# Input projections and GLA of a hybrid diffusion step: from the scheduler's order to an order by program

## The chip, the cores and the metric

The kernel runs on one core of a Trainium2 chip. The metric is device time in microseconds (us) of one execution. Before the change, three runs took 972.02, 972.9 and 973.95 us; the median is 972.9. The engines of a core work side by side, each through its own queue in order: TensorE (PE in the profile, PEld for its weight loads), VectorE (DVE), ScalarE (ACT), GpSimd (POOL), and SyncE (SP), which issues the DMA transfers.

## The reference

One trunk layer for 256 prompt tokens and 1024 latent tokens, width 1024. Each token is RMS-normalised, shifted and scaled by a conditioning vector, and multiplied by one input matrix of 3616 columns. Two head groups read the result.

```python
p = einsum('bld,dp->blp', h, w_in)           # GLA q, k, v, low-rank decays; diff q, k, v; gates
# GLA, forward and backward, chunks of 64 tokens
b = cumsum(g); o = (q * exp(b)) @ S + att @ v            # att: decayed q k^T inside the chunk
S = exp(b_last) * S + (k * exp(b_last - b)).T @ v
# differential attention: two softmax maps per head, keys: cache of 512 + latent (rotary), or prompt
a = softmax(q1 k1) - lam * softmax(q2 k2); o = a @ v
y = x + gate * (concat(rmsnorm(o_gla), rmsnorm(o_diff)) * silu(g)) @ w_out      # then a final rmsnorm
```

Outputs: both token groups, the prompt's diff keys and values, and its two GLA states.

## The kernel before

All float32 products are made from two rounded parts: a tile is split into `hi` (rounded to fp32r) and `lo` (the remainder, rounded), and three matmuls are summed: hi*hi, hi*lo, lo*hi. A weight "unit" is 128 x 1024 values: 128 output features by 1024 inputs, or half of a 256-feature block by tokens.

The program has four stages. The start (`START`, an order written by hand) makes the modulation vectors and the normalised, transposed, split tokens `hhi`, `hlo`, and projects three units. Then come the projections and GLA, which the change rewrites. Attention follows with 16 blocks, again in a hand-written order (`ORDER`), and then the output projection.

The middle part is written as Python generators that `mix` (L102) interleaves by a string: "m" takes one step of the main generator (the projections), "a", "b" and "c" one step of the others. There are three strings, `MIX[0]` to `MIX[2]`. Without `manual_schedule`, this order is only a priority: the framework's scheduler orders each engine's instructions by its own estimate of when they can run. In `START` and `ORDER`, inside `manual_schedule`, TensorE, VectorE, ScalarE and GpSimd execute in the order in which the program issues; SyncE's queue stays with the scheduler in all stages.

- Main steps. `feat_unit` (L462) loads and splits one weight unit and multiplies it with three token blocks of 256, 512 and 512 columns (`feat_block`, L445); it yields after every second of the eight inner tiles for 512 columns, after every fourth for 256. `tok_block` (L518) loads two units and goes over ten tiles of 128 tokens with 256 columns each, in two steps per tile; the first step uses the first unit, the second step the second. Each block ends with a consumer that evicts the accumulator (three buffers, `psA`): `use_kq`, `use_gv`, `use_dv`, `use_dqk` (rotary) and `use_gate` (silu by Abs, Exp, Ln, min and subtract, Exp, multiply).
- `load_unit` (L249) issues the load of a weight unit and its split at the place of use. `WENG` says by which engines: "G" GpSimd alone, "V" GpSimd rounds and VectorE subtracts, "A" ScalarE and GpSimd, "B" ScalarE and VectorE.
- `MIX[0]`, the decay stage: GLA queries and values; beside them `decays` (L982), `modgate` (L695, gate row of the modulation, on VectorE) and `wo_parts` (L681, splitting the output weights in 16 parts and storing them in device memory).
- `MIX[1]`, the gate stage: gates 0 to 3; beside them `pass_a` (L730, forward GLA states, chunk by chunk: multiply on GpSimd, transposes, ScalarE copy, state matmuls) and `cached` (L667, splitting cached keys and values).
- `MIX[2]`: diff values, keys and queries and the gates 4 to 7; beside them the backward GLA pass `pass_b` (L951), the prompt's heads (`prompt`, L992), the loads of the first attention block, and its scores (`first_block`, L1280) through one PSUM buffer.

In `pass_b` a pair of chunks takes eight steps. Step s does `product(s)` on TensorE (`lv`, two double PSUM banks), `grow` (VectorE multiplies, one ScalarE copy) and `select` (VectorE copies where a mask holds). Beside step s, stage s of the pair before is finished: `turn`, `states`, `output`, then `square` and `norm` for each chunk, which read the output `op` from its PSUM bank.

Of the kernel before, what the change touches and what calls it, by code (L numbers as in the profile page):

```python
# [19 lines left out]
P = 128  # L20
D = 1024
# [80 lines left out]
def mix(pattern, main, *others):  # L102
# [4 lines left out]
    for g in gens.values():  # L107
# [14 lines left out]
    ('mmmmabmmmmammammbmammmmamcmmmacbmbbcmmmmcmambcambmcmmmacmmmbcmmmbcmmbmcamamcammbcmmbbcmmabcmmamcammm'  # L122
     'cmmbmm'),
    ('mmamamaaammaaabmmmmaaammaaambmmaammabmabaammaambamammbmmabammmmabammmamamaaaammabaabmaamma'),
    ('ammmmmmammammamaamammammmmaammammmammmamammammmmmammmmaammmmmmammmmammmamamamammmaammammmammmmmmamam'
     'aammmmmamammmammmammammmmmammmmaammmamammmaamammammmmmammammammmmaamammmmaaammmaaaammaaammmmamaamaaa'
     'mmamaaamaammaaamaaammamamamaaamaaamammmaaaamaamaaaaaamaammmmaaamammaammmamm'),
# [51 lines left out]
def body(tc, nc, I, O, ctx):  # L179
# [57 lines left out]
    with psum:  # L237
# [9 lines left out]
        nload = [0]  # L247

        def load_unit(u):  # L249

            raw = wp.tile([P, D], F32, name="w_raw", tag="wr", bufs=2)
            S.dma_start(raw, I["w_u"][u])
            hi = wp.tile([P, D], F32R, name="w_hi", tag="wh")
            lo = wp.tile([P, D], F32R, name="w_lo", tag="wl")
            how = WENG[nload[0]]
            nload[0] += 1
            if how in "AB":
                A.activation(hi, raw, AF.Copy)
            else:
                G.tensor_scalar(out=hi, in0=raw, scalar1=1.0, scalar2=0.0, op0=ALU.mult, op1=ALU.add)  # L260
            (V if how in "BV" else G).tensor_tensor(out=lo, in0=raw, in1=hi.bitcast(F32), op=ALU.subtract)  # L261
            return hi, lo
# [33 lines left out]
        class Start:  # L296
# [146 lines left out]
        sp = proj.enter_context(tc.tile_pool(name="sp", bufs=2, side="right"))  # L443

        def feat_block(w, bi, consumer, s0=0, n=0):  # L445
# [39 lines left out]
        U_LR, U_K, U_Q, U_G, U_DK, U_DQ, U_GV, U_DV = 0, 1, 3, 5, 13, 17, 21, 25  # L485
# [32 lines left out]
        def tok_block(u, consumer, tiles=range(NCH)):  # L518
            w2 = [load_unit(u), load_unit(u + 1)]
            for t in tiles:  # L520
# [3 lines left out]
                for kt in range(KT):  # L524
# [8 lines left out]
                    if kt == 3:  # L533
                        yield
# [4 lines left out]
        def decay(bi, c0, n):  # L539

            nch, ch0 = n // P, c0 // P
            for dr in range(2):
                for pr in range(2):
# [10 lines left out]
                    G.tensor_tensor(out=mn, in0=mn, in1=la, op=ALU.subtract)  # L554

# [55 lines left out]
        def use_dqk(isk, pair, v):  # L611
# [6 lines left out]
            def f(bi, c0, n, ps):  # L618
# [23 lines left out]
                split_store(ua, dst(0), col, n, scale, engine(e + 4))  # L642
# [3 lines left out]
                split_store(ub, dst(1), col, n, scale, engine(e + 4))  # L646
            return f

        def use_gate(m):
            gn = vecs[:, V_GG:V_GG + 1] if m < 4 else vecs[:, V_DG:V_DG + 1]  # L650

            def f(bi, c0, n, ps):
# [6 lines left out]
                A.activation(ls, ls, AF.Exp)  # L659
                gt = sp.tile([P, 512], F32, name="gt", tag="s3")[:, :n]  # L660
                V.scalar_tensor_tensor(out=gt, in0=ps, scalar=gn, in1=ls, op0=ALU.mult, op1=ALU.mult)
                S.dma_start(gt_d[m, :, c0:c0 + n], gt)
                if bi == 0:
                    gated.add(m)
            return f

        def cached():  # L667
            for pair in range(2):
                for v in range(2):
                    r = sp.tile([P, 512], F32, name="kqst", tag="s1")  # L670
                    S.dma_start(r, I["ck"][pair, v])
                    split_store(r, [ks_d[pair][0, v], ks_d[pair][1, v]], 0, PAST, 1.0, G)
                    yield
            for t in range(4):
                r = sp.tile([P, 512], F32, name="kqst", tag="s1")
                S.dma_start(r, I["cv"][t * P:(t + 1) * P])
                rows = vs_d[:, t * P:(t + 1) * P]
                split_store(r, [rows[0], rows[1]], 0, 512, 1.0, G)
                yield

        def wo_parts():  # L681

            for i in range(16):
                m, cs, odd = i // 2, slice(i % 2 * 512, i % 2 * 512 + 512), i % 2
                r = gp.tile([P, 512], F32, name="wor", tag="kk", bufs=2)
                S.dma_start(r, I["w_out"][SLOT[m] * P:(SLOT[m] + 1) * P, cs])
# [6 lines left out]
                yield  # L693

        def modgate():  # L695
# [3 lines left out]
            for kt in range(KT):  # L699
                wg = gp.tile([P, 2, 512], F32, name="wg", tag="att", bufs=2)  # L700
                for hf in range(2):
                    S.dma_start(wg[:, hf], I["w_mod"][kt * P:(kt + 1) * P, 2 * D + hf * 512:2 * D + (hf + 1) * 512])
                for j in range(2):
                    for hf in range(2):
# [8 lines left out]
            for j in range(2):  # L713
                for hf in range(2):
                    cs = slice(hf * 512, (hf + 1) * 512)
                    ps = psL.tile([P, 2, 512], F32, name="gs", tag="lv")[0:1, 0]
                    T.matmul(ps, one, acc[j][hf], start=True, stop=True)
                    row = sp.tile([1, 512], F32, name="grow", tag="s2")
                    S.dma_start(row, I["bgate"][:, cs])
                    V.tensor_tensor(out=row, in0=ps, in1=row, op=ALU.add)  # L720
                    S.dma_start(ga_d[j:j + 1, cs], row)
                    yield
# [7 lines left out]
        def pass_a():  # L730

            cur = None
            for c in range(NCH - 1):
                x = gp.tile([P, 6, 256], F32, name="fa", tag="W", bufs=2)
                k, to, ks, v, kt_ = x[:, 0], x[:, 1], x[:, 2], x[:, 3:5].rearrange("p a b -> p (a b)"), x[:, 5]
                S.dma_start(x[:, 0:1].rearrange("p a (b t) -> p (a b) t", t=P), kq_d[c, :, 0:2])
                S.dma_start(x[:, 1:2].rearrange("p a (b t) -> p (a b) t", t=P), e_d[c, :, 4:6])
                S.dma_start(v, gv_d[c * P:(c + 1) * P])
# [29 lines left out]
        class Pair:  # L768
# [151 lines left out]

            def square(self, i):
                op = self.op[:, :, i * 256:(i + 1) * 256]
                self.sq = gp.tile([P, 512], F32, name="sq")
                A.activation(self.sq.rearrange("p (a b) -> p a b", a=2), op, AF.Square)
                self.sqh = gp.tile([P, 512], F32R, name="sqh", tag="hi")
                G.tensor_scalar(out=self.sqh, in0=self.sq, scalar1=1.0, scalar2=0.0, op0=ALU.mult, op1=ALU.add)
                self.sql = gp.tile([P, 512], F32R, name="sql", tag="lo")
                G.tensor_tensor(out=self.sql, in0=self.sq, in1=self.sqh.bitcast(F32), op=ALU.subtract)

            def norm(self, i):  # L930

                c, rs = 2 * self.p + i, self.sq
                ms = psX.tile([P, 512], F32, name="ms", tag="aux")
                T.matmul(ms, onesr, self.sqh, start=True, stop=False)
# [617 lines left out]
```

## Time and profile before

| | before |
|---|---|
| median of three runs | 972.9 us |
| the profiled execution | 980.17 us, span 978.4 us |
| busy PE / DVE / ACT / POOL | 908.9 / 609.0 / 467.1 / 424.5 us |
| mean granted clock of TensorE | 0.983 |
| DMA | 174.71 MB, mean 179 GB/s |

The span runs from the first to the last instruction. Busy times are shares of that span; idle time of an engine that does not set the pace costs nothing. A matmul's end is modelled, so consecutive matmuls overlap in the record, and the start-to-start distance is the better measure of their pace. The clock is the TensorE clock that was granted: 1.00 is 2.4 GHz and 0.50 is 1.2 GHz.

### The profile page before, as it was taken

To read this page: it belongs to the slowest core of one execution; us is meant where nothing else is said; L and a number is where in the kernel's file an instruction comes from. 1 tells how busy PE (TensorE), PEld (TensorE's weight loads), DVE (VectorE), ACT (ScalarE), POOL (GpSimd) and SP (SyncE) were. 2 spreads that over 40 slices of the span, in tenths; PEclk is the share of its full clock that TensorE was granted. 3 is DMA by queue.
4 is the path that set the end of the run, shared out by engine and by line. 5 is a ranking of instruction groups with operands and counts; after the bars stand their busy time and mean duration, and the time that the engine had idled before them with its cause. 6 is when DMAs were issued, how large, how long until landed. Compare 5 with 4: busy or idle time off the path is not lost. (4 is left out here: it accounts for less than half of the span.)

```text
span 978.4 us, 16000 instructions
## 1 busy us (share of the span) xinstructions
PE 908.9 (93%) x5894; PEld 768.7 (79%) x5894; DVE 609.0 (62%) x837; ACT 467.1 (48%) x893; POOL 424.5 (43%) x349
## 2 busy tenths in 40 slices
PE   6889989899898999889899999899999999999997
PEld 1379878687688988677777888778888888887886
DVE  3688874224337664678766653789999999522223
ACT  2455445525452232324233475678888888521212
POOL 0253544532520312342314300079999999942221
PEclk9889999999999999999999999999999999999999
DMA  7851878788873635255437437397533426037941
GB/s 273 310 173 40 262 230 272 241 270 264 276 244 100 194 120 178 73 168 175 134 120 232 151 121 245 121 312 236 151 99 126 120 71 204 23 108 226 285 130 65
DMA packets 155535, 174.71 MB, mean 179 GB/s; under 512 B 11192, under 2 KB 116792, under 8 KB 155456
## 3 DMA queue, kind: packets, MB, share of 16 engines
q1 hardware_dynamic: 155456, 173.69, 56.1%
q8 instruction: 46, 0.75, 0.4%
q14 instruction: 33, 0.27, 0.1%
HBM read 112.69 MB, written 60.96 MB: 177 GB/s over the span
## 5 line engine op out<-in xcount | busy, mean ns | idle before, releaser
L454 PE MATMUL acc<-hhi,w_hi 128*128 128x512 f32 (+1 forms) x440 | 157.8, 359 | 0.0
L455 PE MATMUL acc<-hlo,w_hi 128*128 128x512 f32 (+1 forms) x440 | 155.6, 354 | 0.0
L456 PE MATMUL acc<-hhi,w_lo 128*128 128x512 f32 (+1 forms) x440 | 155.3, 353 | 0.0
L1153 DVE TENSOR_REDUCE sm<-sc 128x1 f32<-128x1536 f32 x60 | 104.8, 1749 | 9.3 <-PE sc L1146 9.3
L1197 POOL TENSOR_TENSOR aTl<-aT,aTh 128x512 fp32r<-128x512 f32 x80 | 107.7, 1354 | 6.4 <-ACT aTh L1192 1.0
L1146 PE MATMUL sc<-ks,q 128*128 128x512 f32 x360 | 99.4, 412 | 2.7 <-ACT p L1158 2.7
L1158 ACT ACTIVATE p<-sc,sm 128x1536 f32<-128x1536 f32 x60 | 92.6, 1544 | 16.0 <-DVE sm L1153 14.7
L530 PE MATMUL acc<-w_hi,hhi 128*128 128x256 f32 x320 | 94.6, 296 | 6.1 <-ACT kqst L479 4.1
L531 PE MATMUL acc<-w_lo,hhi 128*128 128x256 f32 x320 | 92.7, 290 | 0.9 <-DVE w_lo L261 0.9
L454 PEld LDWEIGHTS acc<-hhi,w_hi 128*128 128x128 f32 x440 | 83.2, 189 | 12.8 <-issue 1.8
L532 PE MATMUL acc<-w_hi,hlo 128*128 128x256 f32 x320 | 92.5, 289 | 0.0
L456 PEld LDWEIGHTS acc<-hhi,w_lo 128*128 128x128 f32 x440 | 83.1, 189 | 11.6 <-issue 0.2
L455 PEld LDWEIGHTS acc<-hlo,w_hi 128*128 128x128 f32 x440 | 83.4, 189 | 10.6 <-issue 0.3
L1194 POOL TENSOR_SCALAR aTh<-aT 128x512 fp32r<-128x512 f32 x64 | 62.4, 975 | 36.1 <-ACT aT L1183 30.3
L1146 PEld LDWEIGHTS sc<-ks,q 128*128 128x128 f32 x360 | 64.0, 191 | 15.1 <-ACT p L1158 3.0
L530 PEld LDWEIGHTS acc<-w_hi,hhi 128*128 128x128 f32 x320 | 63.2, 197 | 12.4 <-ACT kqst L479 4.3
L1168 DVE SCALAR_TENSOR_TENSOR p<-p,sm,p 128x1536 f32<-128x1536 f32 x30 | 70.1, 2338 | 1.1
L1363 PE MATMUL sc<-woh,oh 128*128 128x512 f32 (+1 forms) x168 | 65.0, 387 | 0.9 <-DVE y__9404 L1368 0.9
L1364 PE MATMUL sc<-wol,oh 128*128 128x512 f32 (+1 forms) x168 | 64.5, 384 | 0.0
L1365 PE MATMUL sc<-woh,oh 128*128 128x512 f32 (+1 forms) x168 | 64.5, 384 | 0.0
L531 PEld LDWEIGHTS acc<-w_lo,hhi 128*128 128x128 f32 x320 | 63.2, 198 | 1.6 <-DVE w_lo L261 1.1
L1177 PE MATMUL tp<-ident,p 128*128 128x128 f32 x360 | 58.3, 278 | 6.4 <-DVE p L1168 3.5
(308 smaller groups left out, 2110.3 us busy)
## 6 DMA issues: line engine op xcount, KB each, us to landing
w_raw<-w_u SPq DMA_DIRECT2D x29, 512.0 KB, 5.2
oh<-oh_d SPq DMA_DIRECT2D x20, 512.0 KB, 6.4
wm<-w_mod SPq DMA_DIRECT2D x16, 512.0 KB, 6.4
q<-qs_d SPq DMA_DIRECT2D x64, 128.0 KB, 2.8
ks<-ks_d SPq DMA_DIRECT2D x4, 1536.0 KB, 7.6
vs<-vs_d SPq DMA_DIRECT2D x8, 768.0 KB, 7.5
xt<-x_all SPq DMA_DIRECT2D x10, 512.0 KB, 10.2
x<-x_all SPq DMA_DIRECT2D x10, 512.0 KB, 4.6
```

The lines of the kernel that those rows point to most:

```text
L454: T.matmul(ps, w_h, hhi[bi][:, kt, ts], start=kt == 0, stop=False)
L455: T.matmul(ps, w_h, hlo[bi][:, kt, ts], start=False, stop=False)
L456: T.matmul(ps, w_l, hhi[bi][:, kt, ts], start=False, stop=kt == KT - 1)
L530: T.matmul(ps, h_h, w_h, start=kt == 0, stop=False)
L531: T.matmul(ps, h_h, w_l, start=False, stop=False)
L532: T.matmul(ps, h_l, w_h, start=False, stop=kt == KT - 1)
L1146: T.matmul(sc[:, k0:k0 + w], self.q[:, a, sub, qt * P:(qt + 1) * P], self.ks[:, sub, k0:k0 + w], start=a == 0, stop=a == 1)
L1153: V.tensor_reduce(out=self.sm[qt][:, sub:sub + 1], in_=self.sc[qt, sub], op=ALU.max, axis=AX.X, negate=True)
L1158: A.activation(p_, self.sc.pop((qt, sub)), AF.Exp, bias=sm[:, sub:sub + 1], accum_out=self.s0[:, qt:qt + 1] if sub == 0 else sm[:, 2:3])
L1168: V.scalar_tensor_tensor(out=p0, in0=p1, scalar=cf, in1=p0, op0=ALU.mult, op1=ALU.add)
L1197: eng.tensor_tensor(out=lo, in0=full, in1=hi.bitcast(F32), op=ALU.subtract)
L1363: T.matmul(ps, oh[:, 0, m], woh[m][:, cs], start=m == 0, stop=False)
```

## The change

The whole middle part goes into `manual_schedule`, so the four engines execute it in the order by program, and the three strings are new. The class `Weights` keeps one list of all units: `ask` issues the next load, `split` splits the next unit and asks for another, `take` returns a unit and splits it there if that has not been done. A `feat_unit` splits one unit after its first block, a `tok_block` one at its third tile; the first load and split are put into `START`. `later` holds the second half of an eviction: `turnover` issues one such half before a yield in the middle of a block. `ahead` issues the load of step i+1 before the work of step i, for `cached`, `wo_parts`, `modgate`, and `pass_a` in the same way. Nine of the 16 steps of `wo_parts` move into `MIX[1]`. A `decay` takes two steps. In `pass_b` the output is copied out of PSUM at once (`keep`), both squares are made by ScalarE, and `mean` is a step of its own before `norm`. A prompt head yields three times after its loads, the first attention block's loads four times.

```diff
 MIX = (
+    ('mmmabmmammabmmmambmacmmmbmamcmambmmammcmambmmammambcmmammabmcmammmabmcmammabmmmacmmabmmamcmbmammambm'
+     'acmmmm'),
+    ('mamamabcmmamamabcmmamamabcmmamamabcmmamamamabcmmamamabcmmamamabcmmamamabcmmamamabcmmamam'),
+    ('mmammammammmammammammmammammammmammammammmammammammmammammammmammammammmammammammmammammammmammamma'
+     'mmammmammammammmammammammmammammammmammamamamamamamamamamamamamamamamamamamamamamamamamamamamamamam'
+     'amamamamamamamamamamamamamamamamamamamamamamamamaamamamamamamamm'),
 )
-        def load_unit(u):
...
+        class Weights:
+            def ask(self):
+                if self.asked < len(self.units):
+                    raw = wp.tile([P, D], F32, name="w_raw", tag="wr", bufs=2)
+                    S.dma_start(raw, I["w_u"][self.units[self.asked]])
...
+            def split(self):
...
+                    how = WENG[self.nsplit]
...
+                    self.parts.append((hi, lo))
+                    self.ask()
+            def take(self, u):
+                while not self.parts:
+                    self.split()
+                self.taken += 1
+                return self.parts.pop(0)
+        weights = Weights([U_Q, U_Q + 1, *range(U_GV, U_GV + 4), *range(U_G, U_G + 4), *range(U_DV, U_DV + 4),
+                           *range(U_DK, U_DK + 4), *range(U_DQ, U_DQ + 4), *range(U_G + 4, U_G + 8)])
+            def na(self):
+                weights.ask()
+            def ns(self):
+                weights.split()
+        def turnover():
+            if later:
+                later.pop(0)()
         def feat_block(w, bi, consumer, s0=0, n=0):
                 if kt % YK == YK - 1 and kt < KT - 1 and n > 256 or kt == 3:
+                    turnover()
                     yield
         def feat_unit(u, consumer):
-            w = load_unit(u)
+            w = weights.take(u)
             for bi in range(3):
                 yield from feat_block(w, bi, consumer)
+                if bi == 0:
+                    weights.split()
         def tok_block(u, consumer, tiles=range(NCH)):
-            w2 = [load_unit(u), load_unit(u + 1)]
+            w2 = [weights.take(u), weights.take(u + 1)]
+            for n_, t in enumerate(tiles):
+                if n_ == 2:
+                    weights.split()
         def use_gate(m):
-                A.activation(ls, ls, AF.Exp)
...
+                def rest():
+                    A.activation(ls, ls, AF.Exp)
+                    gt = sp.tile([P, 512], F32, name="gt", tag="s3")[:, :n]
+                    V.scalar_tensor_tensor(out=gt, in0=ps, scalar=gn, in1=ls, op0=ALU.mult, op1=ALU.mult)
+                    S.dma_start(gt_d[m, :, c0:c0 + n], gt)
...
+                later.append(rest)
+        def ahead(n, load, use):
+            nxt = load(0)
+            for i in range(n):
+                yield
+                cur, nxt = nxt, load(i + 1) if i + 1 < n else None
+                use(i, cur)
+            yield
         class Pair:
+            def keep(self):
+                self.o = self.att.rearrange("p a c r t -> p (a c r t)").rearrange("p (i x) -> p i x", i=2)
+                for i in range(2):
+                    A.activation(self.o[:, i].rearrange("p (a b) -> p a b", a=2), self.op[:, :, i * 256:(i + 1) * 256], AF.Copy)
             def square(self, i):
-                A.activation(self.sq.rearrange("p (a b) -> p a b", a=2), op, AF.Square)
+                A.activation(self.sq, self.o[:, i], AF.Square)
-                G.tensor_scalar(out=self.sqh, in0=self.sq, scalar1=1.0, scalar2=0.0, op0=ALU.mult, op1=ALU.add)
+                A.activation(self.sqh, self.o[:, i], AF.Square)
                 G.tensor_tensor(out=self.sql, in0=self.sq, in1=self.sqh.bitcast(F32), op=ALU.subtract)
+            def mean(self, i):
+                self.ms = psX.tile([P, 512], F32, name="ms", tag="aux")
+                T.matmul(self.ms, onesr, self.sqh, start=True, stop=False)
+                T.matmul(self.ms, onesr, self.sql, start=False, stop=True)
-            finish = (lambda y: y.turn(), lambda y: y.states(), lambda y: y.output(), lambda y: y.square(1),
-                      lambda y: y.norm(1), lambda y: y.square(0), lambda y: y.norm(0), lambda y: None)
+            finish = (lambda y: y.turn(), lambda y: y.states(), lambda y: (y.output(), y.keep()), lambda y: y.square(1),
+                      lambda y: y.mean(1), lambda y: (y.norm(1), y.square(0)), lambda y: y.mean(0), lambda y: y.norm(0))
-        mix(MIX[0], seq(*[feat_unit(U_Q + j, use_kq(2 + j)) for j in range(2)],
...
+        with tc.manual_schedule(engines=engines):
+            mix(MIX[0], seq(*[feat_unit(U_Q + j, use_kq(2 + j)) for j in range(2)],
+                    *[tok_block(U_GV + 2 * j, use_gv(j)) for j in range(2)]),
+                decays(), modgate(), few(wo, 8))
+            mix(MIX[1], seq(*[feat_unit(U_G + m, use_gate(m)) for m in range(4)]),
+                seq(pass_a(), few(backward, 1)), cached(), wo)
+            flush()
+            mix(MIX[2], seq(tok_block(U_DV, use_dv(0)), tok_block(U_DV + 2, use_dv(1), range(NCH)),
...
+                seq(backward, stagger([prompt(0), prompt(1)], PL), stagger([prompt(2), prompt(3)], PL), first_loads(), first_block(), prompt_gate()))
+            flush()
```

## Rows read from the trace of the kernel before

**Rows 1.** Stages: length, busy per engine PE, PEld, DVE, ACT, POOL; clock, DMA share, GB/s

```profile
102.00:210.00 108.00, 98.77 (x659) 88.88 (x659) 53.29 (x63) 49.27 (x95) 46.52 (x44) 0.97 0.79 250
210.00:286.00 76.00, 70.81 (x423) 55.88 (x422) 27.39 (x52) 37.11 (x68) 27.37 (x22) 1.00 0.84 275
286.00:380.00 94.00, 89.38 (x836) 83.43 (x835) 60.38 (x97) 27.07 (x53) 18.12 (x12) 0.98 0.45 138
380.00:460.00 80.00, 72.42 (x568) 59.52 (x567) 56.23 (x77) 25.95 (x45) 26.52 (x19) 1.00 0.48 148
460.00:525.00 65.00, 61.10 (x442) 50.50 (x441) 44.15 (x65) 19.45 (x31) 19.89 (x15) 0.97 0.49 154
525.00:625.00 100.00, 98.77 (x543) 84.24 (x542) 58.82 (x93) 55.63 (x121) 16.55 (x14) 1.00 0.54 167
```

**Rows 2.** TensorE's waits, 107 to 645 us: total us, times, longest us

```profile
PE lv L847 <- DVE w L832: 8.3, 8, 3.0
PE ms L934 <- POOL sqh L926: 4.7, 4, 1.6
PE acc L530 <- ACT kqst L479: 4.1, 1, 4.1
...
PE ktp L748 <- POOL fa L739: 2.5, 3, 1.6
...
PE ms L935 <- POOL sql L928: 2.0, 4, 1.2
PE gs L717 <- DVE mn L553: 1.9, 1, 1.9
PE u L873 <- ACT kt L866: 1.4, 1, 1.4
PE acc L530 <- ACT gvst L574: 1.2, 2, 1.0
...
PE acc L531 <- DVE w_lo L261: 0.9, 1, 0.9
```

**Rows 3.** The same columns, for the four microseconds after the longest wait

```profile
142.00:144.00 2.00, 2.00 (x11) 2.00 (x11) 2.00 (x4) 0.93 (x2) 0.11 (x1) 0.50 0.84 237
144.00:146.00 2.00, 1.82 (x10) 1.61 (x9) 1.26 (x2) 0.38 (x1) 0.60 (x1) 0.65 1.02 285
```

**Rows 4.** TensorE's timeline: start us, duration us, instruction

```profile
396.28 0.39 PE L456 MATMUL acc<-hhi,w_lo 128*128 128x512 f32 x1
396.51 0.28 PE L454 MATMUL acc<-hhi,w_hi 128*128 128x256 f32 x1
396.62 0.28 PE L455 MATMUL acc<-hlo,w_hi 128*128 128x256 f32 x1
```

**Rows 5.** Groups by line, 107 to 645 us: count, busy us, mean ns, idle before

```profile
L261 POOL TENSOR_TENSOR w_lo<-w_raw,w_hi 128x1024 fp32r<-128x1024 f32 x12 | 29.8, 2481 | 20.3 <-ACT w_hi L258 19.6
...
L261 DVE TENSOR_TENSOR w_lo<-w_raw,w_hi 128x1024 fp32r<-128x1024 f32 x13 | 18.3, 1405 | 29.2 <-ACT w_hi L258 26.5 <-POOL w_hi L260 2.7
...
L260 POOL TENSOR_SCALAR w_hi<-w_raw 128x1024 fp32r<-128x1024 f32 x11 | 12.8, 1164 | 57.0 <-PE acc L532 51.5 <-DMA w_raw<-w_u 4.6 <-PE acc L455 0.9
L258 ACT ACTIVATE w_hi<-w_raw 128x1024 fp32r<-128x1024 f32 x12 | 12.7, 1060 | 14.3 <-DMA w_raw<-w_u 7.6 <-PE acc L455 6.3 <-DMA px<-vs_d 0.5
...
L656 ACT ACTIVATE la<-la,cst 128x512 f32<-128x512 f32 x15 | 10.9, 727 | 0.4
L658 DVE SCALAR_TENSOR_TENSOR ls<-acc,la 128x512 f32<-128x512 f32 x15 | 10.3, 689 | 23.4 <-ACT la L656 23.3
...
L655 ACT ACTIVATE la<-la 128x512 f32<-128x512 f32 x15 | 9.5, 634 | 0.4
...
L654 ACT ACTIVATE la<-acc 128x512 f32<-128x512 f32 x15 | 9.0, 598 | 20.7 <-PE acc L456 18.7 <-POOL klo L602 2.0
...
L1153 DVE TENSOR_REDUCE sme<-sce 128x1 f32<-128x1536 f32 x4 | 7.0, 1752 | 2.5 <-PE sce L1146 2.5
...
L1158 ACT ACTIVATE pe<-sce,sme 128x1536 f32<-128x1536 f32 x4 | 6.2, 1542 | 5.9 <-DVE sme L1153 5.9
```

More of the change, by code (lines that the diff above doesn't have):

```diff
@@ L658, in f @@
                 V.scalar_tensor_tensor(out=ls, in0=ps, scalar=0.0, in1=la, op0=ALU.min, op1=ALU.subtract)
-                A.activation(ls, ls, AF.Exp)
[L660 to L664, printed above, removed]
-            return f
-        def cached():
[L668 to L679, printed above, removed]
+                def rest():
[3 more added lines that the diff above has]
+                    S.dma_start(gt_d[m, :, c0:c0 + n], gt)
+                    if bi == 0:
+                        gated.add(m)
@@ L681, in wo_parts, with load, use @@
         def wo_parts():
-            for i in range(16):
+            def load(i):
+                m = i // 2
+                return space(I["w_out"][SLOT[m] * P:(SLOT[m] + 1) * P, i % 2 * 512:i % 2 * 512 + 512], "kk", 512)
+            def use(i, r):
                 m, cs, odd = i // 2, slice(i % 2 * 512, i % 2 * 512 + 512), i % 2
-                r = gp.tile([P, 512], F32, name="wor", tag="kk", bufs=2)
-                S.dma_start(r, I["w_out"][SLOT[m] * P:(SLOT[m] + 1) * P, cs])
                 hi = gp.tile([P, 512], F32R, name="wohi", tag=("kt", "sq")[odd])
@@ L692, in wo_parts @@
                 S.dma_start(wo_d[1, m, :, cs], lo.bitcast(F32))
-                yield
+            yield from ahead(16, load, use)
         def modgate():
@@ L698, in modgate, with load @@
             acc = [[ga[:, j, hf] for hf in range(2)] for j in range(2)]
-            for kt in range(KT):
+            def load(kt):
                 wg = gp.tile([P, 2, 512], F32, name="wg", tag="att", bufs=2)
@@ L711, in modgate @@
                                                    in1=acc[j][hf], op0=ALU.mult, op1=ALU.add)
-                yield
[L713 to L722, printed above, removed]
+            yield from ahead(KT, load, use)
+            row = gp.tile([P, 2, 512], F32, name="bg", tag="att", bufs=2)[0:1]
+            S.dma_start(row, I["bgate"].rearrange("p (h f) -> p h f", h=2))
+            sums = []
+            for j in range(2):
+                ps = psL.tile([P, 2, 512], F32, name="gs", tag="lv")[0:1]
+                for hf in range(2):
+                    T.matmul(ps[:, hf], one, acc[j][hf], start=True, stop=True)
+                sums.append(ps)
+                yield
+                out = gp.tile([P, 2, 512], F32, name="grow", tag="E")[0:1]
+                V.tensor_tensor(out=out, in0=ps, in1=row, op=ALU.add)
+                S.dma_start(ga_d[j:j + 1].rearrange("j (h f) -> j h f", h=2), out)
+                yield
         sf_d = dram.tile([NCH, P, 2, P], F32, name="sf_d")
@@ L934, in norm @@
-                T.matmul(ms, onesr, self.sqh, start=True, stop=False)
-                T.matmul(ms, onesr, self.sql, start=False, stop=True)
-                A.activation(rs, ms, AF.Ln, bias=epst)
+                A.activation(rs, self.ms, AF.Ln, bias=epst)
                 A.activation(rs, rs, AF.Exp, scale=-0.5)
-                r3 = rs.rearrange("p (a b) -> p a b", a=2)
-                V.tensor_tensor(out=r3, in0=self.op[:, :, i * 256:(i + 1) * 256], in1=r3, op=ALU.mult)
-                gt = gp.tile([P, 4, P], F32, name="gtc", tag="g")
@@ L976, in pass_b @@
                 last, x = x, nxt
-            for s in range(7):
+            for s in range(8):
                 finish[s](last)
@@ L1006, in prompt @@
                 S.dma_start(q[a][64:P].bitcast(F32), src)
-            yield
+            for _ in range(3):
+                yield
             sc = psL.tile([P, 2, 2, NPR], F32, name="psc", tag="lv")
@@ L1072, in prompt_gate @@
                 S.dma_start(gt[:, h], gt_d[4 + h, :, 0:NPR])
+            yield
+            yield
+            for h in range(4):
                 oc = prompt_o[0][:, h]
@@ L1277, in first_loads @@
             b.load()
-            yield
+            for _ in range(4):
+                yield
         def first_block():
```

110 lines of the change are left out of this document (67 added, 43 removed), and 4 rows, old and new, of the table START.

## The prediction

> **What bounds the kernel now.** I read the busy times by stage first, then TensorE's waits, then the rows of the operations that the change moves. The rewritten part, input projections and gated linear attention (GLA), runs from 102 to 625 us, and TensorE is busy for 90% or more of every stage of it [rows 1]. So a gain has to come out of its gaps: I read the decay stage (102 to 210) with 9.2 us of TensorE idle time, the gate stage (210 to 286) with 5.2, the backward GLA pass in three stretches (286 to 525) with 4.6, 7.6 and 3.9, and the prompt stage (525 to 625) with 1.2. The other engines never fill a stretch: VectorE's fullest is 56.2 of 80 us. The gate stage is peculiar: the DMA engines are busy 0.84 of it at 275 GB/s. The waits [rows 2] name the gaps: GLA products for VectorE (8.3 us), the head-norm matmuls for GpSimd (4.7 and 2.0), one projection tile for ScalarE (4.1), chunk transposes for GpSimd (2.5), and smaller ones.
>
> Two costs hide behind a wait. After the 4.1 us one the granted clock is 0.50 for 2 us and 0.65 for the next 2 [rows 3]; 0.50 is the 1.2 GHz level of two, so 1.0 + 0.7 = 1.7 us of work is lost. And a matmul's recorded end lies past the start of the next: a 128x256 one lasts 0.28 us where the next starts 0.11 later, a 128x512 one 0.39 and 0.23 [rows 4]. So each wait costs some 0.16 us more than its row shows.
>
> A main step ("m") is 6 matmuls at 0.23 or 12 at between 0.11 and 0.12: 1.4 us either way. This is the measure below. The matmuls are the same before and after, so the sum counts gaps alone.
>
> **The change part by part.**
>
> *Own order with even spacing.* In the order by program a GLA step in the backward pass comes after two, at times three, main steps (2.8 to 4.2 us), where before two or three stood side by side. VectorE's chain between two products (two multiplications) fits in that, but rotary and split work is queued on VectorE among them. I take half of the 8.3 us: -4.2. Bounds: 0 and -8.3. The transposed keys that TensorE waits 1.4 for get a step between: -1.4.
>
> *Outputs out of PSUM at once, norm in stages.* ScalarE copies the output (10 copies) and makes the rounded square itself; GpSimd keeps one subtraction, and the mean matmuls come a whole step after the squares. The two norm waits go: -4.7 - 2.0 = -6.7. The added ScalarE work is 10 copies and 10 squares of about 0.6 us, like a gate's absolute value [rows 5], in a pass where ScalarE is busy 27.1 of 94 and 26.0 of 80 us [rows 1]: nothing on the path. If that cover fails, a late copy holds a double PSUM bank, at most what the norm waits cost now (+6.7).
>
> *Loads a step ahead, decays in two steps, evictions in stages.* The 4.1 us wait is an eviction queued on ScalarE behind an exponential that waits for GpSimd; the split decay gives that two main steps. I drop it with the GV eviction (1.2), the modulation sum (1.9) and the transposes that wait for a chunk's load (2.5): -9.7. Bounds: 0, and -9.7 with nothing late next. A deferred gate or key eviction holds its accumulator one main step longer; with three buffers of four main steps each that costs nothing, and if ScalarE falls behind by more, each late block costs its own lateness.
>
> The waits removed are 4.2 + 1.4 + 6.7 + 9.7 = 22.0 us in some 20 places, so 20 x 0.16 = 3.2 more. Low clock goes with them: the granted clock is 0.97 over the 108 us of the decay stage and 0.98 over 94 of the backward pass [rows 1], so 3.2 + 1.9 = 5.1 us of lost work, the size of three such stretches.
>
> *Weights a step ahead: not for token blocks.* A token block takes two weight units, and only the first has been split by then. The second is split at the moment it is taken, and needed after one main step (1.4 us). GV's first block: GpSimd rounds and subtracts, 1.16 + 2.48 - 1.43 = 2.2 us of new wait. Its second block: ScalarE and VectorE, 1.06 + 1.41 - 1.43 = 1.0, no more than that place waits today (0.9 for that subtraction in [rows 2]): 0. DV's first block comes right after the last gate block and the flush, so its ScalarE rounding is queued behind that gate's absolute value, exponential, logarithm, the VectorE minimum and the second exponential: 0.60 + 0.63 + 0.73 + 0.69 + 0.63 (the second exponential taken like the first), then 1.06 and GpSimd's 2.48, less 1.43: 5.4 us [rows 5]. DV's second block: as GV's first, but a slot comes free one main step earlier, 0.8. Sum +8.4. Bounds: 0, if the splitting engines run ahead of TensorE, and 13.8 if in DV's case as much again stands in front (VectorE's first GLA multiplication and the load it waits for are queued there). The two long ones should each bring a low-clock stretch (+3.4); fill +1.0 for six new waits.
>
> *First attention block spaced by single main steps.* Its score matmuls share one PSUM buffer that comes free after the maximum (1.75) and the exponential (1.54). Two main steps (2.8) stand between scores, three beside a combine. One gap is short by 0.5; in another a gate's 1.96 us of ScalarE work starts after one main step, so the exponential ends at 1.4 + 1.96 + 1.54 = 4.9, short by 2.1. +2.6, bounds 0 and 5.
>
> *Output-weight parts moved.* Nine of the 16 go from the decay stage into the gate stage: a load and two stores each of 128x512 f32, 27 x 0.262 = 7.1 MB, beside 275 GB/s x 76 us = 20.9 MB, so 28.0 MB. At the stage's own ratio a full DMA share would be 275 / 0.84 = 327 GB/s: 86 us, of which about 4 can trail into the next stage (share 0.45): +5. Bounds: 0, and 28.0 / 275 = 102 us, +26.
> "DMA: Bandwidth & Descriptors" of the Trainium skill (Specifications) puts the HBM limit of one core at about 358 GB/s. By it the stage would need an estimated 78 us and the move would cost 2 instead of 5, the sum being 3 lower; the 275 GB/s at share 0.84 lie below that limit, and no row here shows the limit itself.
>
> *The rest.* Asking for and splitting the first unit inside the start stage: the split is 3.6 us on GpSimd with three half projections of 1.4 us still to run, so 0, or +1 if late. The prompt heads get two more steps after their loads: 0 to 3, taken as 0, since that stretch keeps TensorE at 98.8 of 100 us.
>
> **Sum:** -22.0 - 3.2 - 5.1 + 8.4 + 3.4 + 1.0 + 2.6 + 5 = -9.9 us. The profiled execution took 980.2 (span 978.4 and 1.8 around it), 7.3 above the median of 972.9. 980.2 - 9.9 = 970.3, and 7.3 less is 963.
>
> **Rivals.**
> 1. *The gate stage becomes DMA-bound (slower).* Cached keys, output weights, chunk loads and gate stores all fall into it, and ScalarE and GpSimd, now strictly in order, stop at the first late load or full store buffer; gate evictions queue behind, then TensorE stops for an accumulator. If the queue gives what it gives now (275 GB/s), the stage takes 102 us: +26 in place of +5, in all 963 + 21 = 984; with 4 us trailing, 980. The change is slower once the stage is longer by 5 + 9.9 = 15 us, that is below 28.0 / 91 = 308 GB/s. For it: the stage already runs at 0.84. Against it: less than 0.5 in the next stage, so some traffic can trail.
> 2. *The new waits are hidden.* Weights are split ahead because GpSimd and ScalarE idle, the DMA fits, the score gaps close: without 8.4 + 3.4 + 1.0 + 2.6 + 5 it is -30, 943. For it: GpSimd is busy 27 of 76 us. Against: in order, the split of DV stands behind an eviction that waits for TensorE's last block.
> 3. *Waits only move.* The steps are at the same counts of main steps as before, and a GLA chain that VectorE paces (100 of 145 us busy from 380 to 525) re-forms its waits: the 10.8 to 12.6 us of products, keys and norms stay, -9.9 + 12 = about no change, 973 to 975.
>
> **Chances.** Forecast (955 to 970) 0.42; hidden waits (below 955) 0.16; no change 0.12; slower 0.30, nearly all of it the first rival. This kernel's measurement can tell about 0.2%, 2 us, from no change. Faster 0.60 (the forecast, the hidden waits and a part of the third rival), same 0.11, slower 0.29. The range runs from 945, the hidden waits without their last 2 us, to 984, the gate stage at today's rate. The likeliest case alone spans 955 to 970.
>
> **What would show it.** In the profile after: no wait of the head-norm matmuls; products wait about 4 us in all; a projection matmul of DV's first block waits some 5 us for GpSimd with a low clock behind; one of GV's about 2; score matmuls of the first block wait 2 to 3; the gate stage shows a DMA share near 1 and 80 us. The prediction is wrong if TensorE's idle time from 102 to 625 us stays above 30 us, or if DV's block does not wait.

## The result and the profile after

The changed kernel takes 1041.3 us (median of 4 runs, 1040.8 to 1042.85) against 973.4 beside it: the ratio is 1.0696, 95% interval 1.0669 to 1.0723. The prediction was 963.0, so its direction was wrong. The profiled execution has a span of 1038.9 us (978.4 before).

Nearly the whole loss lies in the rewritten part. These two rows (stage view: length, busy us of PE, PEld, DVE, ACT, POOL, then clock, DMA share, GB/s) run from its first projection matmul to its last gate matmul, first of the kernel before, then of the changed one.

```profile
102.00:630.00 528.00, 496.22 (x3499) 427.19 (x3499) 303.90 (x450) 217.77 (x419) 154.96 (x125) 0.99 0.60 189
```

```profile
98.00:684.00 586.00, 513.76 (x3497) 438.50 (x3496) 305.02 (x445) 225.26 (x429) 143.25 (x116) 0.94 0.53 169
```

Of the 58.0 us, 40.4 are idle time of TensorE (31.8 became 72.2), and 17.5 are longer busy time of the same matmuls, at a mean clock of 0.94 in place of 0.99 (496.2 became 513.8 us). Attention, behind it, takes 6 us longer (348.6 to 354.7 from its first scores to the end). The part starts 4 us earlier than in the profiled execution before, but that one lies 6.8 us above its median, and `b_fin` below, whose start is that of the kernel before, begins the part at 97.5 us: the changed start need not be what won them. The same view by stages answers to [rows 1]; the last three rows, the end of the backward pass and the prompts, hold 12.5, 17.6 and 12.6 us of the idle time, and the gate stage, the second row, 13.0 (5.2 before).

```profile
98.00:204.00 106.00, 96.46 (x654) 86.22 (x653) 48.39 (x62) 45.00 (x86) 34.25 (x37) 0.95 0.68 210
204.00:287.00 83.00, 70.03 (x386) 54.92 (x385) 23.80 (x44) 40.66 (x76) 35.60 (x30) 0.96 0.84 283
287.00:386.00 99.00, 91.97 (x842) 85.74 (x844) 61.19 (x99) 28.72 (x55) 18.03 (x11) 0.93 0.48 148
386.00:475.00 89.00, 76.47 (x565) 62.88 (x561) 59.87 (x80) 29.77 (x52) 17.69 (x13) 0.92 0.41 127
475.00:568.00 93.00, 75.40 (x514) 61.16 (x513) 55.56 (x75) 29.95 (x51) 26.25 (x18) 0.91 0.43 132
568.00:684.00 116.00, 103.44 (x547) 87.58 (x546) 56.20 (x88) 51.16 (x111) 11.43 (x9) 0.96 0.42 132
```

TensorE's waits from 98 to 700 us in the changed kernel (total us, times, longest), to be held against [rows 2]:

```profile
PE ms L1024 <- ACT sqh L1018: 23.7, 5, 5.8
PE ktp L832 <- POOL fa L823: 10.4, 5, 3.0
PE acc L577 <- ACT w_hi L271: 9.2, 2, 6.2
PE sce L1242 <- ACT pe L1254: 5.3, 2, 4.1
PE lv L931 <- DVE w L916: 5.2, 3, 2.0
PE ms L1025 <- POOL sql L1020: 5.2, 6, 1.3
PE sc L1242 <- DVE gt L712: 4.9, 1, 4.9
PE acc L578 <- POOL w_lo L274: 4.2, 2, 2.4
PE sce L1242 <- DMA q<-qs_d: 3.7, 2, 3.2
```

The head-norm matmuls (`ms`) waited 6.7 us before and wait 28.9 now, though the prediction let them vanish. The timelines of ScalarE, GpSimd, VectorE and TensorE around one such wait show why (start us, duration us, instruction, idle time before it and who ended it):

```profile
359.51 0.67 ACT L1030 ACTIVATE sq<-ms,cst 128x512 f32<-128x512 f32 x1
360.21 0.63 ACT L1031 ACTIVATE sq<-sq 128x512 f32<-128x512 f32 x1
362.90 0.63 ACT L1037 ACTIVATE ohi<-sq 128x512 fp32r<-128x512 f32 x1 [2.06 <-DVE sq L1033]
364.90 0.63 ACT L1016 ACTIVATE sq<-att 128x512 f32<-128x512 f32 x1 [1.37 <-POOL olo L1038]
366.69 0.63 ACT L1018 ACTIVATE sqh<-att 128x512 fp32r<-128x512 f32 x1 [1.16 <-DMA oh_d<-ohi]
367.23 0.37 ACT L639 ACTIVATE vhi<-acc 128x256 fp32r<-128x256 f32 x1
...
363.61 1.26 POOL L1038 TENSOR_TENSOR olo<-sq,ohi 128x512 fp32r<-128x512 f32 x1 [10.70 <-ACT ohi L1037]
367.56 1.30 POOL L1020 TENSOR_TENSOR sql<-sq,sqh 128x512 fp32r<-128x512 f32 x1 [2.69 <-DMA oh_d<-olo]
...
367.63 0.42 DVE L640 TENSOR_TENSOR vlo<-acc,vhi 128x256 fp32r<-128x256 f32 x1 [4.76 <-ACT vhi L639]
...
362.01 0.28 PE L579 MATMUL acc<-w_hi,hlo 128*128 128x256 f32 x1
...
367.38 0.79 PE L1024 MATMUL ms<-sqh,onesr 128*128 128x512 f32 x1 [3.99 <-ACT sqh L1018]
368.91 0.79 PE L1025 MATMUL ms<-sql,onesr 128*128 128x512 f32 x1 [0.75 <-POOL sql L1020]
```

In one step `finish` now does `norm(1)` and then `square(0)`, and both use the single buffers `sq`, "hi" and "lo". So ScalarE stops three times: for VectorE's two products, for GpSimd to finish reading `sq`, and for a store of `ohi` to land; GpSimd waits for the store of `olo`. From 359.51 to 368.86 this takes 9.3 us, and one step, about 4 us, lies before `mean(0)`. Meanwhile the eviction `vhi`, whose accumulator got its last matmul at 362.01, stands behind ScalarE's squares until 367.23, and VectorE idles 4.76 us behind it. The clock around it (same columns as the first rows above; answers to [rows 3]):

```profile
363.00:365.00 2.00, 0.38 (x8) 0.19 (x4) 0.00 (x0) 0.63 (x2) 1.26 (x1) 1.00 0.34 97
365.00:367.00 2.00, 0.00 (x0) 0.00 (x0) 0.00 (x0) 0.84 (x2) 0.00 (x0) 0.67 0.99 296
367.00:369.00 2.00, 0.88 (x2) 0.38 (x2) 1.37 (x2) 0.59 (x2) 1.30 (x1) 0.50 0.22 72
369.00:371.00 2.00, 2.00 (x9) 1.90 (x9) 1.30 (x3) 0.63 (x1) 0.00 (x0) 0.50 0.18 59
```

### The profile page after: what moved, and what is told of

Read it like the earlier page. It is cut to its first block, busy times and chain, and to the rows that moved or that the text cites. A ratio compares the mean times of both kernels' runs of the same rounds, so it can differ in the third digit from the quotient of the medians.

```text
span 1038.9 us, 15962 instructions
## 1 busy us (share of the span) xinstructions
PE 926.7 (89%) x5894; PEld 780.2 (75%) x5894; DVE 609.8 (59%) x835; ACT 478.7 (46%) x913; POOL 413.0 (40%) x339
## 4 chain that ended last, share of the span: by engine, by line
PE 49%; DVE 20%; issue 13%; DMA 8%; POOL 5%; ACT 4%; SPq 1%; POOLq 0%; ACTq 0%; DVEq 0%
DVE p L1264 6%; DVE sm L1249 5%; PE sc L1242 4%; PE sc L1463 4%; PE sc L1464 4%; PE sc L1465 4%; PE acc L497 3%; PE acc L498 3%; PE acc L499 3%; PE acc L577 3%; PE acc L578 3%; PE acc L579 3%; PE lv L931 3%; PE tp L1273 2%; PE op L999 2%
## 5 line engine op out<-in xcount | busy, mean ns | idle before, releaser
L497 PE MATMUL acc<-hhi,w_hi 128*128 128x512 f32 (+1 forms) x440 | 164.6, 374 | 0.2 <-ACT w_hi L271 0.2
L499 PE MATMUL acc<-hhi,w_lo 128*128 128x512 f32 (+1 forms) x440 | 159.3, 362 | 0.8 <-DVE w_lo L274 0.8
L498 PE MATMUL acc<-hlo,w_hi 128*128 128x512 f32 (+1 forms) x440 | 159.9, 363 | 0.0
L1249 DVE TENSOR_REDUCE sm<-sc 128x1 f32<-128x1536 f32 x60 | 104.8, 1749 | 10.3 <-PE sc L1242 10.3
L1242 PE MATMUL sc<-ks,q 128*128 128x512 f32 x360 | 102.0, 420 | 7.1 <-DVE gt L712 4.9
L1254 ACT ACTIVATE p<-sc,sm 128x1536 f32<-128x1536 f32 x60 | 92.6, 1543 | 17.5 <-DVE sm L1249 12.7
L497 PEld LDWEIGHTS acc<-hhi,w_hi 128*128 128x128 f32 x440 | 87.2, 198 | 14.5 <-issue 2.4
L499 PEld LDWEIGHTS acc<-hhi,w_lo 128*128 128x128 f32 x440 | 86.8, 197 | 13.6 <-DVE w_lo L274 1.0
L498 PEld LDWEIGHTS acc<-hlo,w_hi 128*128 128x128 f32 x440 | 87.0, 198 | 10.8
```

What stands on the lines that cost most here:

```text
L1242: T.matmul(sc[:, k0:k0 + w], self.q[:, a, sub, qt * P:(qt + 1) * P], self.ks[:, sub, k0:k0 + w], start=a == 0, stop=a == 1)
L1249: V.tensor_reduce(out=self.sm[qt][:, sub:sub + 1], in_=self.sc[qt, sub], op=ALU.max, axis=AX.X, negate=True)
```

## The experiments

Times are medians; each ratio is against runs of the kernel before on the same chip (972.6 to 974.7 us).

### The norm chain

`n_order` puts one more step between `norm(1)` and `mean(0)`:

```diff
-  lambda y: y.mean(1), lambda y: (y.norm(1), y.square(0)), lambda y: y.mean(0), lambda y: y.norm(0))
+  lambda y: (y.mean(1), y.norm(1)), lambda y: y.square(0), lambda y: y.mean(0), lambda y: y.norm(0))
```

> The changed kernel with one edit: the last steps of a chunk pair are mean(1) with norm(1) in step 4, square(0) in step 5, mean(0) in step 6, norm(0) in step 7, so that a whole step more lies between norm(1) and mean(0). Theory N (the norm chain of chunk 0 takes 9.3 us from the Ln of norm(1) to the end of sql, with one step of about 4 us before TensorE wants it): the ms waits on ScalarE's sqh (23.7 us) and GpSimd's sql (5.2 us) fall below 10 us together, and with the low clock that follows each of them the time falls by 25 to 38 us, to 1003 to 1016. Rival O (the written order of the engines itself, or VectorE's masks, pace the backward pass, and the norm wait only shows where it surfaces): another wait of the same size takes its place, lv on VectorE for one, and the time stays within 1033 to 1045.

Measured: 1024.2 us, ratio 1.0488 (1.043 to 1.0546), 17 us won, between the two forecasts: the `ms` waits are 12.7 us, not below 10, and the products' waits rise from 5.2 to 9.0 us, a part of what rival O expected. `n_bufs` keeps the step but does `square(0)` ahead of `norm(1)` and gives the two different places; idle space holds them (the pair totals `t` after step 2, the keys' "kt"):

```diff
-  lambda y: y.square(1),
+  lambda y: (y.square(1, x or y), y.gates(1)),          # gates: the load of gtc
...
-  lambda y: (y.norm(1), y.square(0)),
+  lambda y: (y.square(0), y.norm(1), y.gates(0)),
...
+  sq = host.t[:, 0:512] if host else gp.tile([P, 512], F32, name="sq")
+  hi = gp.tile([P, 4, P], F32R, name="ohi", tag=("hi", "kt")[i])
+  lo = rs.bitcast(F32R).rearrange("p (m t) -> p m t", m=4) if i else gp.tile([P, 4, P], F32R, name="olo", tag="lo")
```

> The changed kernel with the same steps, but the squares of chunk 0 come before norm(1) in step 5 and stand in a buffer of their own, and norm(1)'s outputs in places that are idle then, so that sq, sqh and sql of chunk 0 wait for nothing of norm(1). Theory N: mean(0) finds its operands, the 5 waits of 3.8 to 5.8 us go, the time falls by 25 to 38 us to 1003 to 1016. If the spacing alone were at fault and not the shared buffers, this run would gain and the one with the moved step as well, by the same; if ScalarE's and GpSimd's own work in step 5 is too long whatever it waits for, this run keeps more than half of the 23.7 us. Rival O: 1033 to 1045.

Measured: 1011.8 us, ratio 1.0368 (1.03 to 1.0436): 29.5 us won. Of the `ms` waits only 3.0 us are left, while the products' waits rise to 9.5. Theory N holds for nearly half of the loss. Order inside the step, buffers and the place of the gate loads are changed together here, so their shares are not told apart. The waits that now lead:

```profile
PE ktp L832 <- POOL fa L823: 11.4, 5, 3.8
PE lv L931 <- DVE w L916: 9.5, 5, 3.5
PE acc L577 <- ACT w_hi L271: 8.8, 2, 5.8
```

### The order against the parts

`sched` is the changed kernel without `with tc.manual_schedule(...)` around the three `mix` calls; `b_manual` is the kernel before with it.

> The changed kernel without the written engine order: the scheduler orders the projections and GLA again, all else as changed (strings, loads ahead, weights a step ahead, deferred parts, steps of finish). Theory N with order as its condition: the scheduler lets evictions pass the blocked squares, and the time is 965 to 995. Rival P (the parts are at fault: where the second weight halves, the wo parts and the squares stand): it stays at 1020 to 1045.

> The kernel before with the written engine order alone: its own strings and its own code, engines in program order. Theory N says nothing of it. If a written order as such costs (in-order queues with evictions and products of one step behind each other, nothing staged for it), it is 1000 or more, worse than the changed kernel, whose stages then were needed; if the order costs nothing and the rest of the change is to blame, it is 968 to 985.

Measured: `sched` 976.5 us, ratio 1.0023 (0.9995 to 1.0051); `b_manual` 1201.35, ratio 1.2308 (1.2242 to 1.2375). So the written order costs 65 us on the new code and 228 on the old. The new strings, stages and early loads together make it far cheaper (which of them does is not tested), and in the scheduler's order all these other parts together are worth no measurable difference. TensorE's first 3298 matmuls of 5894 stand in the same order in `sched` and in the changed kernel, eight of the ten norm means among them; yet the last product of the backward pass, inside that stretch, starts at 497.3 us in place of 531.1. ScalarE's timeline in `sched` at the place shown above:

```profile
344.99 0.63 ACT L1016 ACTIVATE sq<-att 128x512 f32<-128x512 f32 x1 [1.42 <-POOL olo L1038]
345.53 0.36 ACT L639 ACTIVATE vhi<-acc 128x256 fp32r<-128x256 f32 x1
345.79 0.62 ACT L913 ACTIVATE kk<-w 128x512 f32<-128x512 f32 x1
346.85 0.63 ACT L1018 ACTIVATE sqh<-att 128x512 fp32r<-128x512 f32 x1 [0.44 <-DMA oh_d<-ohi]
```

The eviction `vhi` and the keys' copy `kk` pass `sqh` while its buffer's store lands, so VectorE and TensorE go on; `sched` keeps 14.6 us of `ms` waits.

### The other waits

`n_gate`, `n_wts` and `n_all` start from `n_bufs`:

```diff
 n_gate, n_all
-  G.tensor_tensor(out=ks, in0=k, in1=to, op=ALU.mult)
+  V.tensor_tensor(out=ks, in0=k, in1=to, op=ALU.mult)
 n_wts, n_all
-  if bi == 0:
+  if bi == 0 or bi == 1 and u in (U_Q + 1, U_G + 3):
       weights.split()
-  st = sp.tile([P, 256], F32, name="gvst", tag="s1")      # in use_gv
+  st = sp.tile([P, 256], F32, name="gvst", tag="h1")
```

> n_bufs (1011.8) with one edit: the chunk multiply of the forward GLA pass on VectorE in place of GpSimd, whose queue holds the cached parts, the wo parts and the weight split ahead of it. Theory Q (the in-order GpSimd queue makes the transposes ktp late): the 11.4 us of ktp waits fall below 3, the low clock after them goes as well, and the time falls by 8 to 15 us to 997 to 1004. Rival D (the gate stage is bound by its transfers, whose share is 0.75 to 0.90 there): the waits turn up on the loads of the chunks or on the weights, and the time stays within 3 us of 1011.8.

> n_bufs with the second weight halves of GV's and DV's first blocks split a feature block earlier (units GV1 and DV1), and with the GLA value staging in a buffer kind of its own, so that ScalarE's decay does not wait there for a store to land ahead of GV3's split. Theory W (splits on the spot, behind an in-order ScalarE): the waits 2.35 (GV1), 5.8 and 0.9 (GV3), 3.0 and 2.0 (DV1) fall from 14 us together to 4 or less (GV3's own split stays), and with the low clock after GV3 and DV1 the time falls by 10 to 17 us to 995 to 1002. Rival: the stores' landing is not what holds GV3 up, and only the first and the last two go: 1002 to 1006.

> n_bufs with both edits, of n_gate and of n_wts. If the three causes are separate, the gains add: 18 to 32 us below 1011.8, 980 to 994. If an in-order schedule only passes its waits on to the next place, the sum of the two gains is not reached by more than 5 us.

Measured: `n_wts` 1000.9 us, 10.8 won, as theory W has it; the waits on weight halves fall from 14.1 to 3.5 us. In the changed kernel ScalarE shows how GV's second block came to wait 6.2 us: the decay's Abs waits for a staging buffer, shared with the GV eviction, whose store must land, and the weight rounding stands behind it. (`n_wts` mends this and the late splits in one run, so the two are not told apart.)

```profile
164.04 0.69 ACT L597 ACTIVATE la<-z,vecs 128x512 f32<-128x512 f32 x1 [2.46 <-DMA gv_d<-gvst]
...
166.05 1.04 ACT L271 ACTIVATE w_hi<-w_raw 128x1024 fp32r<-128x1024 f32 x1
```

`n_gate` took 1008.4 us, 3.4 won, and theory Q missed. It had GpSimd's queue right, as the changed kernel's rows show (GpSimd and then TensorE):

```profile
225.07 1.30 POOL L758 TENSOR_TENSOR wolo<-r,wohi 128x512 fp32r<-128x512 f32 x1
226.34 1.05 POOL L273 TENSOR_SCALAR w_hi<-w_raw 128x1024 fp32r<-128x1024 f32 x1
227.47 2.34 POOL L274 TENSOR_TENSOR w_lo<-w_raw,w_hi 128x1024 fp32r<-128x1024 f32 x1
229.77 0.72 POOL L823 TENSOR_TENSOR fa<-fa 128x256 f32<-128x256 f32 x1
...
230.55 0.44 PE L832 MATMUL ktp<-ident,fa 128*128 128x128 f32 x2 [2.97 <-POOL fa L823]
```

But on VectorE the multiply stands behind a gate's minimum, which waits for ScalarE's logarithm; the 11.4 us of `ktp` waits became 10.3 (`n_all`, VectorE and then TensorE):

```profile
207.19 0.69 DVE L707 SCALAR_TENSOR_TENSOR ls<-acc,la 128x512 f32<-128x512 f32 x1 [3.29 <-ACT la L705]
207.80 0.41 DVE L823 TENSOR_TENSOR fa<-fa 128x256 f32<-128x256 f32 x1
...
208.36 0.41 PE L832 MATMUL ktp<-ident,fa 128*128 128x128 f32 x2 [1.95 <-DVE fa L823]
```

So `n_all`, 1000.3 us, far from the 980 to 994 of separate causes, gets nothing measurable beyond `n_wts`.

### Whose order costs

All six leave engines of the middle part to the scheduler by the set given to `manual_schedule`; five start from `n_bufs`. In each, the orders of the engines that keep the written one are the same to the instruction. SyncE's order of transfers is the scheduler's in every run and changes in all six; no run holds it fixed. TensorE's own waits for transfers do not account for the gains: 3.3 us in `n_bufs`, 5.7 in `pe_only`.

```diff
-  with tc.manual_schedule(engines=engines):          # PE, DVE, Activation, Pool
+  engines={DVE, Activation, Pool}     pe_free
+  engines={PE}                        pe_only;  a_pe_only: the same on the changed kernel
+  engines={PE, DVE, Pool}             act_free
+  engines={PE, Activation, Pool}      dve_free
+  engines={PE, DVE, Activation}       pool_free
```

> n_bufs (1011.8) with TensorE left to the scheduler; VectorE, ScalarE and GpSimd keep the written order to the instruction. Of the 49 us between n_bufs and s_bufs (962.4), theory T (the loss is on TensorE: an instruction whose operand is late stands in front of projection matmuls that are ready, one step of the strings being shorter than the chains on the other engines) expects two thirds or more to come back: 962 to 979. Rival E (the written order of ScalarE, VectorE and GpSimd makes the operands themselves late) expects less than a third: 996 or more.

> The other half: TensorE keeps the written order of n_bufs to the instruction, VectorE, ScalarE and GpSimd are left to the scheduler. Theory T: 996 to 1012, little comes back. Rival E: 962 to 979. In between for both runs, the two orders wait on each other and neither is the cause alone.

| written order on | buffers as changed | own buffers (`n_bufs`) |
|---|---|---|
| all four engines | 1041.3 | 1011.8 |
| all but TensorE (`pe_free`) | | 998.1 |
| TensorE alone (`a_pe_only`, `pe_only`) | 982.8 | 969.7 |
| none (`sched`, `s_bufs`) | 976.5 | 962.4 |

Theory T, which I had written first, falls, and rival E has both runs. `pe_only` is at 0.9975 of the kernel before (0.9957 to 0.9993): TensorE's written order costs 7.3 us when the others are free (13.7 when they are not, by `pe_free`), and the order of the three other engines costs 42.1. With `pe_only`, `ktp` waits 1.6 us and the weight rounding 2.6, at unchanged places on TensorE:

```profile
PE acc L577 <- ACT w_hi L271: 2.6, 1, 2.6
...
PE ktp L832 <- DVE Sf L842: 1.6, 1, 1.6
```

> n_bufs (1011.8) with ScalarE alone left to the scheduler, the other orders the same to the instruction. Theory A (ScalarE is the queue that everything passes: evictions, gate activations, squares and weight halves, and what is blocked there holds up the rest): 20 to 42 us come back, 970 to 992. Rival J (the three orders are late together, one waiting on the next): each of the three runs brings 15 us or less, 997 or more.

> n_bufs with VectorE alone left to the scheduler. Theory A: 1000 to 1012. If VectorE's order is the cause (the waits lv 9.5 us, ktp after the move to VectorE 10.3 us and the gates at the start of attention 4.7 us are all of it), 970 to 992. Rival J: 997 or more here and in the two others.

> n_bufs with GpSimd alone left to the scheduler. It can take the chunk multiply past the cached and wo parts: at most the 11.4 us of ktp waits and some low clock, of which n_gate got 3.4 us; 1000 to 1010 under every theory but one in which GpSimd's order is the cause, 970 to 992.

> The changed kernel, buffers as they were, with TensorE alone in the written order. If the shared buffers of the norm chain are a cause of their own (they lengthen the chain from norm(1) to mean(0) under any order, and TensorE's place for mean(0) is fixed), it stands 15 to 30 us above pe_only (969.7): 985 to 1000. If they hurt only because ScalarE and GpSimd could not run anything else meanwhile, 970 to 980.

Released one at a time from 1011.8, ScalarE brings 14.8 us (997.0, ratio 1.0234, 1.0213 to 1.0255), VectorE 18.2 (993.6, 1.02, 1.0173 to 1.0227) and GpSimd 11.3 (1000.5, 1.0273, 1.0245 to 1.03). Together 44.2, about what all three bring at once (42.1): theory A falls, and no single engine is the culprit. These runs stand on four chips; by the ratios in place of the times the three bring 13, 16 and 9 us, all three at once 38, and TensorE 11, so the picture is the same. Rival J's sizes fit but for VectorE's, which is above its bound; its reason, engines late together, does not follow, since the shares add. That each engine loses by instructions queued behind one that waits is shown above at single places (`vhi` on ScalarE, the chunk multiply on GpSimd and on VectorE) and argued for the rest. GpSimd brings 11.3 us though it is at most 43% busy in any stage of the changed kernel.

`a_pe_only` is at 1.0088 (1.0067 to 1.0109), 13.1 us above `pe_only`, between its two forecasts; with no order written the difference is 14.1. So 13 to 14 of `n_bufs`' 29.5 us are the cost of the shared buffers also where ScalarE, VectorE and GpSimd are free. The other 16 appear only while ScalarE, VectorE and GpSimd keep the written order; that they come from what stood behind the blocked squares, as `vhi` did, is argued and not shown apart.

### A version better than both

`s_bufs` is `sched` with `n_bufs`' chain, `b_fin` the kernel before with that chain alone, `s_all` is `s_bufs` with the edits of `n_all`.

> The kernel with the scheduler's order (sched, 976.5) and n_bufs' norm chain. There TensorE waits 14.6 us for ms (sqh 4.2, sql 10.4). Theory N (shared buffers make the norm chain long under any order): these fall below 4 and the time to 962 to 970, below the kernel before. If the scheduler already hid the chain but for its own placing of sql, nothing moves: 974 to 979.

> The kernel before, in the scheduler's order, with only the end of a chunk pair as in n_bufs: copy out of PSUM at once, squares on ScalarE, mean and norm in steps of their own, buffers of their own. If the gain of s_bufs over before (11.4 us) comes from the norm chain alone, this is 960 to 967. If it comes from the rest of the change (loads and weights a step ahead, split parts), this is 970 to 976; TensorE waited only 6.7 us for ms in before, which with its low clock bounds this edit's gain near 10.

> s_bufs (962.4) with both edits of n_all, in the scheduler's order. s_bufs waits 2.6 us for the weight part on ScalarE, 1.5 us for ktp and 0.8 us for w_lo; if the edits take these away the time is 956 to 961. If the scheduler places around them what it placed before, 960 to 965.

Measured: `s_bufs` 962.4 us, ratio 0.986 (0.9805 to 0.9915); `b_fin` 967.1, ratio 0.9935 (0.9906 to 0.9963), just past its band, so the norm chain gives about half of `s_bufs`' gain, though the two intervals just overlap; `s_all` 956.7, ratio 0.9836 (0.981 to 0.9862), the lowest of all. Its interval overlaps that of `s_bufs`, so that its two edits add to the gain is not shown. Its middle part, first projection to last gate:

```profile
98.00:607.00 509.00, 490.97 (x3509) 426.61 (x3507) 312.69 (x453) 226.72 (x436) 143.91 (x107) 0.99 0.62 196
```

TensorE idles 18.0 us there, against 31.8 before and 72.2 in the changed kernel, at the clock of before.

## Why the prediction was wrong, point by point

- **"Own order with even spacing", -5.6.** Products went from 8.3 to 5.2 us (-3.1), the keys from 1.4 to 0.7. That was in part luck: TensorE was held at the norm matmuls then, and where these waits are mended, at the same spacing, products wait 9.0 us (`n_order`) and 9.5 (`n_bufs`), more than before. What the sum left out was the rest of the order: only DV's split was charged for what stands ahead of it.
- **"Outputs out of PSUM at once, norm in stages", -6.7: the step that failed.** The waits became 28.9 us, +22.2. I followed `mean` back to `square`, a step apart, and not `square(0)` back to `norm(1)`, one line ahead of it in the same buffers. The bound on a failure, "at most what the norm waits cost now (+6.7)", was none: a wait of a chain is bounded by the chain (9.3 us), five times over.
- **"Loads a step ahead", -9.7.** The 4.1, 1.2 and 1.9 us went. In `sched`, with the same parts, the two evictions wait again (4.0 and 1.7 us), so the parts alone did not remove them. The 2.5 us of `ktp` became 10.4, behind GpSimd's other work.
- **"Weights a step ahead: not for token blocks", +8.4.** GV's first block 2.35 (said 2.2) and DV's 3.01 + 1.84 = 4.85 (said 5.4) are right, and by the predicted chain: Abs, exponential, logarithm, minimum, second exponential, rounding, then 2.34 us of subtraction. GV's second block, set to 0 from the bare durations, waits 6.2 + 0.9, where it waited 1.7 before; DV's second, put at 0.8, does not wait.
- **"First attention block", +2.6, bounds 0 and 5.** Its scores wait 5.3 us for ScalarE and 3.7 for the late query loads; the deferred last gate costs 4.9 more at the start of attention.
- **"Low clock", -5.1 + 3.4.** The busy time grew by 17.5 us in place of shrinking by 1.7, since there were more and longer waits.
- **Rival 1, the gate stage DMA-bound.** It had the sign and not the cause. From the last GV to the first DV matmul, before takes 72.8 us, the changed kernel 79.6, `sched` 70.0, `n_bufs` 81.3 and `pool_free` 72.3 with the three other engines' order unchanged. `pool_free` moves in 72.5 us (row below) what `n_bufs` moves in 81, some 22 MB: the transfers fit in, and GpSimd's queue was what lengthened the stage. It made 7 of the 68 us. The sum's own +5 for this stage ("Output-weight parts moved") is near that by luck: it was worked out from 28.0 MB of transfers.

```profile
202.00:274.50 72.50, 66.44 (x383) 52.35 (x383) 22.83 (x42) 38.08 (x72) 35.49 (x29) 1.00 0.91 307
```

- **My own test** (wrong if TensorE's idle time from 102 to 625 us stays above 30 us) came out at 72.2 over the whole part; its other half, that DV's block waits, held.

The norm chain is 29.5 of the 68 us. The larger rest is a term that the sum does not have: the written order on ScalarE, VectorE and GpSimd, put at nothing beyond DV's split, still cost 42.1 us with the chain mended. It was treated as a saving with a few exceptions, though the scheduler's order lets ready work pass what waits, as `vhi` and `kk` do in `sched`.

"Perfetto Trace Analysis" of the Trainium skill (Sequencer Loop) has an engine instruction pushed into its engine's queue, where it waits for its semaphores. The rows agree: `vhi`, its accumulator full since 362.3, starts behind `sqh` at 367.23.

## What to carry to other kernels

Before an order is fixed on an engine, list for each instruction what stands ahead of it there and what that waits for, a landing store and a shared buffer included; a wait costs everything behind it, on engines that are half idle too. Two stages of a pipeline that share a single buffer belong one full chain apart, or in separate buffers, and here idle space for these was found in tiles that were dead by then. When a scheduler is available, test "order" and "parts" apart first: here the parts, with their waits mended, were worth 1.6% in the scheduler's order, and the written order cost 5 to 7%.

## What the runs showed of the hardware

A wait much shorter than the 4 us ones can lower the clock too. After the 1.95 us one in `n_all` (TensorE's clock is the third number from the end) it is 0.80, 0.50 (the 1.2 GHz level) and 0.85 in the next three stretches, 0.2 + 0.5 + 0.15 of 2 us each, so an estimated 1.7 us of work lost on top of 1.95:

```profile
206.00:208.00 2.00, 0.41 (x2) 0.00 (x0) 0.81 (x2) 1.13 (x3) 0.00 (x0) 1.00 0.91 257
208.00:210.00 2.00, 1.64 (x7) 1.39 (x8) 0.96 (x2) 1.74 (x4) 0.21 (x1) 0.80 0.58 235
210.00:212.00 2.00, 2.00 (x7) 1.52 (x6) 0.00 (x0) 0.23 (x1) 2.00 (x2) 0.50 0.74 276
212.00:214.00 2.00, 2.00 (x14) 1.34 (x13) 0.26 (x1) 0.00 (x0) 0.30 (x1) 0.85 1.01 378
```

Not every such wait does: right after the 2.97 us one that ends at 230.55 in the changed kernel (shown above) the clock stays at 1.00.

```profile
230.00:232.00 2.00, 1.45 (x8) 1.22 (x9) 0.00 (x0) 0.93 (x3) 0.49 (x1) 1.00 1.03 389
```

The last row of `n_all` also shows 378 GB/s at a full DMA share, above the 358 that the prediction weighed. "Perfetto Trace Analysis" of the Trainium skill (Roofline) says that a core alone can pass that share, up to about 435 GB/s; this row agrees with it.
